# Two decoder layers on one core: gate and up of every feed-forward group token-major, the activations turned in squares of 32 and sent round by DRAM

## The chip, the cores and the metric

The kernel runs as one program on one core of a Trainium2 chip. Its time is the device time of one execution in microseconds (us); a comparison uses the median of several executions. A profile is one further execution, recorded by the hardware profiler; its span is the stretch from the first to the last recorded work.

## The reference

Two layers of a decoder trunk on 256 tokens of width 1024, all in fp32. Each layer has two feed-forward blocks (FFN), so the kernel runs four of them, and the change lies in these:

```python
D_MODEL, SEQ, DEPTH, D_FF = 1024, 256, 2, 2816

def swiglu(x, w_gu, w_down):
    gate, up = jnp.split(x @ w_gu, 2, axis=-1)      # (256, 2816) each
    return (jax.nn.silu(gate) * up) @ w_down        # (256, 1024)

def hybrid_layer(...):
    h = layer_norm(ALPHA * x + 0.5 * swiglu(x, ffn1_w_gu, ffn1_w_down), ...)
    # token mixers on h @ w_in: gated DeltaNet, sliding-window attention, memory cross-attention
    ...
    h = layer_norm(ALPHA * h + merged @ w_out, ...)
    return layer_norm(ALPHA * h + 0.5 * swiglu(h, ffn2_w_gu, ffn2_w_down), ...)
```

## The kernel before

**Precision.** Every large product is made of three float32r products. An operand x is split into hi (a cast, on ScalarE, `split` L116) and lo = x - hi (a subtraction, on VectorE, L117); the product is hi*hi + hi*lo + lo*hi (`mm3`).

**The weight stream.** All weights lie in one DRAM array `wst` in the order of use. `unit` takes the next 128 x 1024 piece (512 KB): a DMA on SP's queue into one of 3 `raw` buffers, then the split into one of 5 pairs `whi`, `wlo`. The buffers set how far the stream runs ahead: a new DMA starts when VectorE has done with a `raw` buffer, a new cast when TensorE has done with a `whi` buffer.

**PSUM.** The pool `acc` has four banks of 128 x 512, used in turn.

**An FFN.** The 2816 gate and 2816 up columns go in 22 tiles of 128, or 11 groups of 256 (group i holds tiles 2i and 2i + 1). Group 0 is made ahead of the rest, by `both` (first FFN) or `first` (the other three), token-major: for each block tb of 128 tokens one bank holds 256 gate and 256 up columns, the activations hT are the stationary operand and 512 weight columns move. `first_out` then applies silu, multiplies, turns the 128 x 256 result by two TensorE transposes and splits it into the tile `u0`. Tiles 2 to 21 go through `shares`, feature-major: 128 weight columns are stationary and the activations move. hT holds hi and lo side by side (128 x 512), so `whi` times both is one matmul of 512 columns, and `wlo` times hi is one of 256. For every k of 8 and for gate and up that makes 2 matmuls of 512 and 2 of 256. Two copies and two additions join the halves of the banks (L183, L184), then come silu (L372), the product (L374) and the split into `u`. The result is feature-major, as the down projection wants its stationary operand, and nothing leaves the core for it. The down projection (`projA`) reads 22 units and accumulates into all four `acc` banks and one more.

**Order.** A scheduler of the recording layer orders each engine's instructions by priorities; the loads on SP's queue keep program order. An engine executes its instructions in the order recorded, so an instruction that waits holds back all that stand behind it on that engine. GpSimd (POOL) is idle in the FFN but for eight DMAs of the memory rows (`mdr`, L431 and L435). In the token mixers it issues the DMAs `dr<-t` and `w<-dr`, which send a tile round by DRAM.

Of the kernel before, what the change touches and what calls it, by code (L numbers as in the profile page):

```python
# [38 lines left out]
def tile_trunk(ctx, tc, x, xT, mem, wst, lnp, memln, cvw, rows, cst, out):  # L39
    nc = tc.nc  # L40
# [5 lines left out]
    p2 = ctx.enter_context(tc.tile_pool(name="p2", bufs=2))  # L46
# [4 lines left out]
    pd = ctx.enter_context(tc.tile_pool(name="pd", bufs=2, space=bass.MemoryType.DRAM))  # L51
    uid = [0]

    def nm(s):
        uid[0] += 1
        return f"{s}_{uid[0]}"

    def T(pool, shape, tag, dt=F32, bufs=None):
        kw = {} if bufs is None else {"bufs": bufs}
        return pool.tile(shape, dt, tag=tag, name=nm(tag), **kw)  # L60

    def acc():
        return T(psA, [P, 512], "acc")
# [4 lines left out]
    def sm():  # L68
        return T(psS, [P, 512], "sm")
# [6 lines left out]
    ident = cs[:, C_ID:C_ID + P]  # L76
# [22 lines left out]
    def unit(w=U, dst=None, cuts=1, behind=None):  # L99
        ahead = tc.high_priority(offset=AHEAD) if pos[0] >= 8 * P * U else nullcontext()  # L100
        raw = T(praw, [P, U], "raw")
        src = wst[pos[0]:pos[0] + P * w].rearrange("(p w) -> p w", p=P)
        pos[0] += P * w
        (ph, th), (pl, tl) = dst or ((phi, "whi"), (plo, "wlo"))
        with ahead:
            hi = T(ph, [P, U], th, F32R)
            lo = T(pl, [P, U], tl, F32R)
            for i in range(cuts):
                c = slice(i * w // cuts, (i + 1) * w // cuts)
                nc.sync.dma_start(raw[:, c], src[:, c])  # L110
                with tc.issue_after(behind) if behind else nullcontext():
                    split(hi[:, c], lo[:, c], raw[:, c])
        return hi, lo

    def split(hi, lo, src):
        nc.scalar.copy(hi, src)  # L116
        return nc.vector.tensor_tensor(lo, src, hi.bitcast(F32), op=ALU.subtract).ins  # L117
# [3 lines left out]
    def pe(ins):  # L121

        return tc.keep_in_program_order(ins) if pinned[0] else ins

    def matmul(*a, **k):
        return pe(nc.tensor.matmul(*a, **k))  # L126
# [4 lines left out]
    def mm3(o, l, r, first, last, skip=False):  # L131
        (lh, ll), (rh, rl) = l, r
        matmul(o, lh, rh, start=first, stop=False, skip_group_check=skip)
        matmul(o, lh, rl, start=False, stop=False, skip_group_check=skip)
        matmul(o, ll, rh, start=False, stop=last, skip_group_check=skip)
# [28 lines left out]
            yield  # L164
        return banks

    def shares(hT, behind=None):


        banks = [acc() for _ in range(2)]  # L170
        for uu in range(2):
            hi, lo = unit(behind=behind)
            for kk in range(4):
                k = uu * 4 + kk
                cs_ = [slice((kk * 2 + t) * P, (kk * 2 + t + 1) * P) for t in range(2)]

                for t in range(2):
                    matmul(banks[t], hi[:, cs_[t]], hT[2][:, k], start=k == 0, stop=False, skip_group_check=True)
                for t in range(2):
                    matmul(banks[t][:, 0:S], lo[:, cs_[t]], hT[0][:, k, :], start=False, stop=k == KD - 1, skip_group_check=True)  # L180
        y = T(p2, [P, 2, S], "t2", bufs=4)
        for t in range(2):
            nc.scalar.copy(y[:, t], banks[t][:, S:])  # L183
            nc.vector.tensor_tensor(y[:, t], y[:, t], banks[t][:, 0:S], op=ALU.add)  # L184
        return y

    def halves(xt, use):

        for i in range(2):
            (b,) = yield from projB_parts(xt, 2, 4)  # L190
            use(i, b)
# [42 lines left out]
    def full_rows():  # L234

        a, b, c, d = (acc() for _ in range(4))
        return [[a, b], [c, d[:, 0:S], at()[:, 0:S]]]
# [8 lines left out]
    def new_hT():  # L246

        t = T(pu, [P, KD, 2, S], "hT", F32R)
        return t[:, :, 0, :], t[:, :, 1, :], t
# [64 lines left out]
    class Ffn:  # L314
# [27 lines left out]
        def both(self, hT):  # L342
            self.bank = {tb: acc() for tb in range(2)}
            for k in range(KD):
                hi, lo = self.units[k // 2]
                c = slice((k % 2) * 512, (k % 2) * 512 + 512)
                for tb in range(2):
                    ts = slice(tb * P, (tb + 1) * P)
                    mm3(self.bank[tb], (hT[0][:, k, ts], hT[1][:, k, ts]), (hi[:, c], lo[:, c]), k == 0, k == KD - 1)
            for tb in range(2):  # L350
                self.first_out(tb)

        def first_out(self, tb):
            ps = self.bank[tb]
            hf = self.glu(ps[:, 0:S], ps[:, S:2 * S])
            pt = sm()
            for j in range(2):
                nc.tensor.transpose(pt[:, j * P:(j + 1) * P], hf[:, j * P:(j + 1) * P], ident)
            ts = slice(tb * P, (tb + 1) * P)
            split(self.h(0)[:, 0, :, ts], self.h(0)[:, 1, :, ts], pt[:, 0:S].rearrange("p (j t) -> p j t", j=2))  # L360

        def glu(self, g, u):
            sg = T(p2, [P, S], "t2", bufs=4)
            nc.scalar.activation(sg, g, AF.Silu)
            hf = T(p2, [P, S], "t2", bufs=4)
            nc.vector.tensor_tensor(hf, sg, u, op=ALU.mult)
            return hf

        def rest(self, hT, tail, dsts, post, mid={}, behind=None):
            for f in range(2, NFT):  # L370
                y = shares(hT, behind if f == 2 else None)
                nc.scalar.activation(y[:, 0], y[:, 0], AF.Silu)  # L372
                hf = y[:, 1]
                nc.vector.tensor_tensor(hf, y[:, 0], hf, op=ALU.mult)  # L374
                t = self.h(f // 2)
                split(t[:, 0, f % 2, :], t[:, 1, f % 2, :], hf)
                if f in mid:
                    mid[f]()
            outs = full_rows()
            projA((lambda k: self.hu[k // 2][:, 0, k % 2, :], lambda k: self.hu[k // 2][:, 1, k % 2, :]), D, 1, NFT, outs, tail, dsts, after=post)  # L380

# [32 lines left out]
    def begin(nxt, hT):  # L414
        nxt.first(hT, 0)
        nxt.first(hT, 1)
        nxt.first_out(0)
        nxt.first_out(1)


    mdr = T(pd, [4, P, 1024], "mdr", bufs=1)
# [569 lines left out]
    hT = new_hT()  # L991
# [20 lines left out]
    for l in range(NL):  # L1012
        mT = []
        mid = memory_T(mT, l)
# [16 lines left out]
        if not last:  # L1031
            f1, hT = Ffn(), post.hT
# [4 lines left out]
def _kcols(w, kpu):  # L1037

    k = w.shape[0] // P
    return np.ascontiguousarray(w.reshape(k // kpu, kpu, P, w.shape[1]).transpose(0, 2, 1, 3)).ravel()  # L1040


def _stream(i):
    parts = []
    for l in range(NL):
        def ffn(gu, dn):
            parts.append(_kcols(np.concatenate([gu[:, 0:S], gu[:, FF:FF + S]], 1), 2))
            g = gu.reshape(KD // 4, 4, P, 2, NFT, P)
            parts.append(np.ascontiguousarray(g[:, :, :, :, 2:].transpose(4, 0, 2, 1, 3, 5)).ravel())
            parts.append(_kcols(dn, 1))  # L1050
        ffn(i["ffn1_w_gu"][l], i["ffn1_w_down"][l])
        mk = i["w_mem_kv"][l]
        parts.append(_kcols(mk[:, :512], 2))
        parts.append(_kcols(mk[:, 512:], 2))
        w = i["w_in"][l]
        parts.append(_kcols(np.concatenate([w[:, 1536:2056], w[:, 2696:2824]], 1), 1))
        for s in (512, 0, 1024, 2824):
            parts.extend(_kcols(w[:, c:c + 256], 4) for c in (s, s + 256))
        parts.append(_kcols(w[:, 2568:2696], 8))
        sq = w[:, 2056:2568].reshape(D, 2, 4, 64).transpose(0, 2, 1, 3).reshape(D, 512)  # L1060
        parts.extend(_kcols(sq[:, s:s + 256], 4) for s in (0, 256))
        wb = i["w_branch"][l]
# [57 lines left out]
```

## Time and profile before

| | us |
|---|---|
| median of 3 runs (1297.15 to 1299.23) | 1298.52 |
| the profiled execution | 1298.02 |
| its span | 1296.2 |
| what lies around the span | 1.8 |
| TensorE busy in it | 1277.9 |
| VectorE, ScalarE, GpSimd busy | 888.4, 708.5, 77.2 |

A timeline row gives start, duration, engine, source line, operation, output<-inputs (moving operand ahead of the stationary one for a matmul), the shape and how many instructions were merged. A matmul's duration includes its way through the array and overlaps the next one; what a matmul costs is the distance from start to start. In a row of instruction groups the two numbers behind the first bar are the busy time in us and the mean of one in ns; behind the second stands the idle time ahead of them, with what ended it.

### The profile page before, as it was taken

The page shows a single profiled execution, that of the slowest core. Times are in us where ns is not written, and L with a number is a line of the kernel's source. Part 1 is how long each engine was busy: PE and PEld are TensorE (multiplying, and loading weights), DVE is VectorE, ACT ScalarE, POOL GpSimd, SP SyncE. Part 2 cuts the span into 40 slices and gives each one's busy share as a digit, 9 for nine tenths or more (in the row PEclk, how much of TensorE's full clock was granted, in tenths as well). Part 3 has the DMA queues.
Part 4 walks back from the last instruction along what each step waited for, and adds up shares of the span by engine and source line. Part 5 has one row for each costly group of instructions (what it writes and reads, how often), then busy time and mean ns, then how long its engine had stood idle before and what let it go on. Part 6 is the DMA issues. An engine that isn't in the chain of part 4 may idle for free.

```text
span 1296.2 us, 20444 instructions
## 1 busy us (share of the span) xinstructions
PE 1277.9 (99%) x7832; PEld 1116.2 (86%) x7832; DVE 888.4 (69%) x1430; ACT 708.5 (55%) x1177; POOL 77.2 (6%) x135
## 2 busy tenths in 40 slices
PE   8999999999999999999999999999999999999997
PEld 6888889999878888888888888899988788888886
DVE  6787556796647777665677674759867388777645
ACT  6656444666674546554455654456656654565541
POOL 0000000102311000000000000000033100000000
PEclk9999999999999999999999999999999999999999
DMA  7867564654533636555665555556453256455553
GB/s 266 276 210 244 193 229 128 220 174 135 161 131 130 228 129 211 191 185 192 228 222 200 188 186 192 199 175 201 163 165 131 98 182 224 149 194 194 189 189 111
DMA packets 68577, 240.25 MB, mean 185 GB/s; under 512 B 8160, under 2 KB 9312, under 8 KB 68480
## 3 DMA queue, kind: packets, MB, share of 16 engines
q1 hardware_dynamic: 66176, 232.53, 53.1%
q0 software_dynamic: 2304, 6.43, 1.8%
q8 instruction: 61, 1.00, 0.3%
q14 instruction: 36, 0.29, 0.1%
HBM read 235.64 MB, written 3.28 MB: 184 GB/s over the span
## 4 chain that ended last, share of the span: by engine, by line
PE 89%; DVE 4%; DMA 4%; ACT 2%; issue 1%; SPq 0%; DVEq 0%; ACTq 0%
PE acc L126 78%; PE at L126 4%; DMA raw<-in_wst_dram 3%; PE sm L126 3%; PE sm L129 1%; ACT whi L116 1%; DVE wlo L117 1%; PE acc L340 1%; PE acc L337 1%; DMA pp<-in_mem_dram 1%; PE acc L338 1%; PE at L129 1%; DVE bnst L282 0%; DVE u L117 0%; DVE h L301 0%
## 5 line engine op out<-in xcount | busy, mean ns | idle before, releaser
L117 DVE TENSOR_TENSOR wlo<-raw,whi 128x1024 fp32r<-128x1024 f32 (+2 forms) x403 | 487.4, 1214 | 308.7 <-ACT whi L116 307.2
L116 ACT CAST whi<-raw 128x1024 fp32r<-128x1024 f32 (+2 forms) x403 | 414.4, 1033 | 366.7 <-DMA raw<-in_wst_dram 99.0
L126 PE MATMUL acc<-hT,whi 128*128 128x512 f32 (+1 forms) x1952 | 524.9, 357 | 0.0
L126 PEld LDWEIGHTS acc<-hT,wlo 128*128 128x128 f32 x1616 | 304.6, 189 | 56.0
L126 PE MATMUL acc<-hT,wlo 128*128 128x256 f32 x1616 | 347.6, 279 | 0.0
L126 PEld LDWEIGHTS acc<-hT,whi 128*128 128x128 f32 x1952 | 299.8, 190 | 0.2
L126 PE MATMUL acc<-whi,u 128*128 128x512 f32 (+1 forms) x800 | 246.7, 373 | 0.0
L126 PEld LDWEIGHTS acc<-whi,u 128*128 128x128 f32 x800 | 150.1, 188 | 27.7 <-DVE t L184 1.2
L126 PE MATMUL acc<-whi,hT 128*128 128x512 f32 (+1 forms) x544 | 168.4, 380 | 5.6 <-ACT whi L116 5.6
L126 PE MATMUL acc<-wlo,u 128*128 128x512 f32 (+1 forms) x400 | 148.4, 371 | 0.0
L126 PEld LDWEIGHTS acc<-whi,hT 128*128 128x128 f32 x544 | 100.6, 189 | 23.7 <-ACT whi L116 5.6
L126 PE MATMUL acc<-wlo,hT 128*128 128x512 f32 (+1 forms) x272 | 101.9, 375 | 0.0
L126 PEld LDWEIGHTS acc<-wlo,u 128*128 128x128 f32 x400 | 75.5, 189 | 12.2
L372 ACT ACTIVATE t<-t 128x256 f32<-128x256 f32 x80 | 33.4, 417 | 60.4 <-DVE t L184 59.9
L184 DVE TENSOR_TENSOR t<-t,acc 128x256 f32<-128x256 f32 x160 | 59.9, 415 | 0.0
L126 PEld LDWEIGHTS acc<-wlo,hT 128*128 128x128 f32 x272 | 51.5, 190 | 8.2 <-DVE wlo L117 0.9
L183 ACT COPY t<-acc 128x256 f32<-128x256 f32 x160 | 51.5, 369 | 0.1
L116 ACT CAST u<-t 128x256 fp32r<-128x256 f32 x80 | 32.1, 401 | 20.4 <-DVE t L374 20.4
L374 DVE TENSOR_TENSOR t<-t 128x256 f32<-128x256 f32 x80 | 33.9, 424 | 9.2 <-ACT t L372 7.7
L126 PE MATMUL at<-whi,u 128*128 128x256 f32 x152 | 39.0, 283 | 0.0
L117 DVE TENSOR_TENSOR u<-t,u 128x256 fp32r<-128x256 f32 x80 | 33.6, 420 | 7.1 <-ACT u L116 7.1
L489 DVE SCALAR_TENSOR_TENSOR t<-acc,cw,t 128x255 f32<-128x255 f32 (+2 forms) x72 | 34.5, 479 | 0.9
(248 smaller groups left out, 1250.4 us busy)
## 6 DMA issues: line engine op xcount, KB each, us to landing
raw<-in_wst_dram SPq DMA_DIRECT2D x409, 512.0 KB, 3.6
raw<-in_wst_dram SPq DMA_DIRECT2D x16, 324.0 KB, 3.0
gB<-in_lnp_dram SPq DMA_DIRECT2D x6, 512.0 KB, 6.4
bB<-in_lnp_dram SPq DMA_DIRECT2D x6, 512.0 KB, 5.9
mdr<-w POOLq DMA_DIRECT2D x4, 512.0 KB, 6.8
w<-dr POOLq DMA_DIRECT2D x4, 512.0 KB, 8.8
w<-mdr POOLq DMA_DIRECT2D x4, 512.0 KB, 5.2
t<-in_xT_dram SPq DMA_DIRECT2D x4, 256.0 KB, 5.3
```

The costliest lines, as they stand in the source:

```text
L116: nc.scalar.copy(hi, src)
L117: return nc.vector.tensor_tensor(lo, src, hi.bitcast(F32), op=ALU.subtract).ins
L126: return pe(nc.tensor.matmul(*a, **k))
L129: return pe(nc.tensor.transpose(*a))
L183: nc.scalar.copy(y[:, t], banks[t][:, S:])
L184: nc.vector.tensor_tensor(y[:, t], y[:, t], banks[t][:, 0:S], op=ALU.add)
L337: nc.tensor.matmul(ps, hT[0][:, k, ts], hi[:, c], start=k == 0, stop=False)
L338: nc.tensor.matmul(ps, hT[0][:, k, ts], lo[:, c], start=False, stop=False)
L340: nc.tensor.matmul(ps, hT[1][:, k, ts], hi[:, c], start=False, stop=k == KD - 1)
L372: nc.scalar.activation(y[:, 0], y[:, 0], AF.Silu)
L374: nc.vector.tensor_tensor(hf, y[:, 0], hf, op=ALU.mult)
L489: nc.vector.scalar_tensor_tensor(yc[:, j, d:], b[:, j, :S - d], w[:, t:t + 1], yc[:, j, d:], op0=ALU.mult, op1=ALU.add)
```

## The change

All groups are now made as group 0 was, token-major, with 512 weight columns moving: per k and token block the three matmuls of `mm3`. `shares` is gone. For each group the new `out` makes silu and product of both token blocks into one tile t, which holds 32 columns of block 0 beside the same 32 columns of block 1, and so on. VectorE then transposes every 32 x 32 square of t in place of TensorE (L341). That leaves the four bands of 32 partitions each with the wrong quarter of the tokens; four DMAs of GpSimd's queue write the bands to a DRAM tile `tr`, 64 KB each in pieces of 512 bytes (L345), and a fifth, which waits for the four, reads it back with 2 KB to a partition (L346). The result y is split into `u`. The rows of the down weights are reordered on the host to fit, and so is the stream; the number and size of the stream's units are the same, and SP's queue stands in the same order.

```diff
-    def shares(hT, behind=None):
-        banks = [acc() for _ in range(2)]
-        for uu in range(2):
-            hi, lo = unit(behind=behind)
-            for kk in range(4):
...
-                for t in range(2):
-                    matmul(banks[t], hi[:, cs_[t]], hT[2][:, k], start=k == 0, stop=False, skip_group_check=True)
-                for t in range(2):
-                    matmul(banks[t][:, 0:S], lo[:, cs_[t]], hT[0][:, k, :], start=False, stop=k == KD - 1, skip_group_check=True)
...
+            self.out(0, self.bank)
+
+        def out(self, i, banks):
+            t = T(p2, [P, 8, 2, 32], "t2", bufs=4)
             for tb in range(2):
-                self.first_out(tb)
...
+                g, u = (banks[tb][:, c:c + S].rearrange("p (j x) -> p j x", j=8) for c in (0, S))
+                nc.scalar.activation(t[:, :, tb, :], g, AF.Silu)
+                nc.vector.tensor_tensor(t[:, :, tb, :], t[:, :, tb, :], u, op=ALU.mult)
+            z = T(p2, [P, 512], "t2", bufs=4)
+            nc.vector.transpose(z, t.rearrange("p j t x -> p (j t x)"))
+            y = T(p2, [P, 512], "t2", bufs=4)
+            d = T(pd, [4, 32, 4, P], "tr")
+            for q in range(4):
+                nc.gpsimd.dma_start(d[:, :, q].rearrange("b c x -> c b x"), z[32 * q:32 * q + 32].rearrange("c (b x) -> c b x", b=4))
+            nc.gpsimd.dma_start(y, d.rearrange("b c q x -> (b c) (q x)"))
+            hi, lo = (self.h(i)[:, n].rearrange("p a (t q s) -> p (a t) q s", t=2, q=4) for n in range(2))
+            split(hi, lo, y.rearrange("p (q n s) -> p n q s", q=4, n=4))

         def rest(self, hT, tail, dsts, post, mid={}, behind=None):
-            for f in range(2, NFT):
-                y = shares(hT, behind if f == 2 else None)
-                nc.scalar.activation(y[:, 0], y[:, 0], AF.Silu)
...
+            for i in range(1, NFT // 2):
+                banks = [acc() for _ in range(2)]
+                for uu in range(KD // 2):
+                    hi, lo = unit(behind=behind if i == 1 and uu < 2 else None)
+                    for kk in range(2):
+                        k, c = 2 * uu + kk, slice(kk * 512, kk * 512 + 512)
+                        for tb in range(2):
+                            ts = slice(tb * P, (tb + 1) * P)
+                            mm3(banks[tb], (hT[0][:, k, ts], hT[1][:, k, ts]), (hi[:, c], lo[:, c]), k == 0, k == KD - 1)
+                self.out(i, banks)
```

In the orders below a number behind a name is the buffer; rows are of the second FFN (end of layer 0). ScalarE before, tiles 12 and 13: the copies, the silu and the cast of one tile, then the next.

```order
L183 COPY t_929_5491<-acc_5445 128x256
L183 COPY t_929_5491<-acc_5446 128x256
L372 ACTIVATE t_929_5491<-t_929_5491 128x256
L116 CAST whi_5637<-raw_5636 128x1024
L116 CAST u_930_5498<-t_929_5491 128x256
L116 CAST whi_5670<-raw_5669 128x1024
L183 COPY t_939_5547<-acc_5501 128x256
```

Each cast into `u` reads what the same engine and VectorE have just made. ScalarE now, group 9 and the start of group 10 (t_971 is the y of group 8, t_988 the t of group 9):

```order
L338 ACTIVATE t_988_5488<-acc_5414 128x8x32
L116 CAST whi_5602<-raw_5601 128x1024
L116 CAST u_973_5411<-t_971_5404 128x512
L338 ACTIVATE t_988_5488<-acc_5415 128x8x32
L116 CAST whi_5623<-raw_5622 128x1024
L116 CAST whi_5644<-raw_5643 128x1024
L116 CAST whi_5665<-raw_5664 128x1024
L338 ACTIVATE t_1007_5579<-acc_5505 128x8x32
```

The cast of group 8's y, which waits for a DMA, now stands between the two silus of group 9. VectorE before, tile 14 of that FFN:

```order
L184 TENSOR_TENSOR t_948_5602<-t_948_5602,acc_5556 128x256
L184 TENSOR_TENSOR t_948_5602<-t_948_5602,acc_5557 128x256
L374 TENSOR_TENSOR t_948_5602<-t_948_5602 128x256
L117 TENSOR_TENSOR wlo_5749<-raw_5747,whi_5748 128x1024
L117 TENSOR_TENSOR u_949_5609<-t_948_5602,u_949_5609 128x256
L117 TENSOR_TENSOR wlo_5782<-raw_5780,whi_5781 128x1024
```

The residual into `u` belongs to the tile just made. VectorE now, groups 9 and 8:

```order
L339 TENSOR_TENSOR t_988_5488<-t_988_5488,acc_5414 128x8x32
L117 TENSOR_TENSOR wlo_5603<-raw_5601,whi_5602 128x1024
L117 TENSOR_TENSOR u_973_5411<-t_971_5404,u_973_5411 128x512
L339 TENSOR_TENSOR t_988_5488<-t_988_5488,acc_5415 128x8x32
L341 STREAM_TRANSPOSE t_989_5493<-t_988_5488 128x512
L117 TENSOR_TENSOR wlo_5624<-raw_5622,whi_5623 128x1024
```

The residual of group 8 stands ahead of group 9's second product and of its transpose. GpSimd now, groups 8, 9 and 10 (nothing stood here before):

```order
L345 DMA tr_5405<-t_970_5402 32x4x128 x4
L346 DMA t_971_5404<-tr_5405 128x512
L345 DMA tr_5496<-t_989_5493 32x4x128 x4
L346 DMA t_990_5495<-tr_5496 128x512
L345 DMA tr_5587<-t_1008_5584 32x4x128 x4
L346 DMA t_1009_5586<-tr_5587 128x512
```

t_971 and t_990 are the y of groups 8 and 9, which ScalarE casts; each read stands behind its four writes, and the next group's writes behind it. TensorE now, just behind the second FFN's group 10: the start of its down projection, from the seventh matmul on (six into `acc_5596` and `acc_5597` stand ahead):

```order
L126 MATMUL acc_5598<-whi_5602,u_821_4683 128x512
L126 MATMUL acc_5598<-wlo_5603,u_821_4683 128x512
L126 MATMUL acc_5598<-whi_5602,u_821_4683 128x512
L126 MATMUL at_5600<-whi_5602,u_821_4683 128x256
L126 MATMUL at_5600<-wlo_5603,u_821_4683 128x256
L126 MATMUL at_5600<-whi_5602,u_821_4683 128x256
L126 MATMUL acc_5596<-whi_5623,u_821_4683 128x512
L126 MATMUL acc_5596<-wlo_5624,u_821_4683 128x512
L126 MATMUL acc_5596<-whi_5623,u_821_4683 128x512
L126 MATMUL acc_5597<-whi_5623,u_821_4683 128x512
L126 MATMUL acc_5597<-wlo_5624,u_821_4683 128x512
L126 MATMUL acc_5599<-whi_5602,u_821_4683 128x256
```

`acc_5598` and `acc_5599` take the two banks of group 10. So 17 matmuls, 14 of 512 columns and 3 of 256, stand between the end of group 10 and the first into `acc_5599`, which can start only when VectorE has read group 10's second bank for its second product.

More of the change, by code (lines that the diff above doesn't have):

```diff
@@ L165, in projB_parts @@
         return banks
-    def shares(hT, behind=None):
-        banks = [acc() for _ in range(2)]
-        for uu in range(2):
-            hi, lo = unit(behind=behind)
-            for kk in range(4):
-                k = uu * 4 + kk
-                cs_ = [slice((kk * 2 + t) * P, (kk * 2 + t + 1) * P) for t in range(2)]
-                for t in range(2):
-                    matmul(banks[t], hi[:, cs_[t]], hT[2][:, k], start=k == 0, stop=False, skip_group_check=True)
-                for t in range(2):
-                    matmul(banks[t][:, 0:S], lo[:, cs_[t]], hT[0][:, k, :], start=False, stop=k == KD - 1, skip_group_check=True)
[L181 to L185, printed above, removed]
     def halves(xt, use):
@@ L349, in both @@
                     mm3(self.bank[tb], (hT[0][:, k, ts], hT[1][:, k, ts]), (hi[:, c], lo[:, c]), k == 0, k == KD - 1)
+            self.out(0, self.bank)
+        def out(self, i, banks):
+            t = T(p2, [P, 8, 2, 32], "t2", bufs=4)
             for tb in range(2):
-                self.first_out(tb)
[L353 to L367, printed above, removed]
-        def rest(self, hT, tail, dsts, post, mid={}, behind=None):
-            for f in range(2, NFT):
-                y = shares(hT, behind if f == 2 else None)
[L372 to L378, printed above, removed]
+                g, u = (banks[tb][:, c:c + S].rearrange("p (j x) -> p j x", j=8) for c in (0, S))
@@ new lines, in out @@
+            nc.gpsimd.dma_start(y, d.rearrange("b c q x -> (b c) (q x)"))
+            hi, lo = (self.h(i)[:, n].rearrange("p a (t q s) -> p (a t) q s", t=2, q=4) for n in range(2))
+            split(hi, lo, y.rearrange("p (q n s) -> p n q s", q=4, n=4))
+        def rest(self, hT, tail, dsts, post, mid={}, behind=None):
+            for i in range(1, NFT // 2):
[8 more added lines that the diff above has]
+                self.out(i, banks)
+                for f in (2 * i, 2 * i + 1):
+                    if f in mid:
+                        mid[f]()
@@ L416, in begin @@
         nxt.first(hT, 1)
-        nxt.first_out(0)
-        nxt.first_out(1)
+        nxt.out(0, nxt.bank)
     mdr = T(pd, [4, P, 1024], "mdr", bufs=1)
@@ L1046, in ffn @@
         def ffn(gu, dn):
[L1047 to L1050, printed above, removed]
+            for c in range(0, FF, S):
+                parts.append(_kcols(np.concatenate([gu[:, c:c + S], gu[:, FF + c:FF + c + S]], 1), 2))
+            parts.append(_kcols(dn.reshape(FF // S, 4, 2, 32, D).transpose(0, 2, 1, 3, 4).reshape(FF, D), 1))
         ffn(i["ffn1_w_gu"][l], i["ffn1_w_down"][l])
```

## Prediction

> **What bounds the kernel now.** I read the page's head, the granted clock, the chain and then TensorE's waits.
>
> ```profile
> span 1296.2 us, 20444 instructions
> PE 1277.9 (99%) x7832; PEld 1116.2 (86%) x7832; DVE 888.4 (69%) x1430; ACT 708.5 (55%) x1177; POOL 77.2 (6%) x135
> PEclk9999999999999999999999999999999999999999
> PE 89%; DVE 4%; DMA 4%; ACT 2%; issue 1%; SPq 0%; DVEq 0%; ACTq 0%
> PE acc L126 <- ACT whi L116: 5.6, 1, 5.6
> PE sm L129 <- DVE h L301: 1.9, 4, 1.0
> ```
>
> TensorE is busy 99% of the span at full clock, and 89% of the chain is its own. The last two rows are the longest of its waits: the first is the start of the kernel, and nothing behind it adds up to more than a few us. So two things count: how long TensorE's own instructions take, and whether the change makes it wait. The work taken from ScalarE and VectorE (copies, additions) is worth nothing by itself, since TensorE hides it already.
>
> **TensorE's stream.** A timeline of TensorE gives each form's price from start to start. The first two rows are the first and last whole k of the second FFN's `shares` behind its transposes, 153 k apart; the next two are the form that the change uses everywhere (hT stationary, weights moving, in the order of `both`), 27 matmuls apart.
>
> ```profile
> 480.65 0.63 PE L126 MATMUL acc<-hT,whi 128*128 128x512 f32 x2
> 587.24 0.63 PE L126 MATMUL acc<-hT,whi 128*128 128x512 f32 x2
> 11.60 0.63 PE L126 MATMUL acc<-whi,hT 128*128 128x512 f32 x2
> 17.73 0.62 PE L126 MATMUL acc<-whi,hT 128*128 128x512 f32 x2
> 475.90 0.38 PE L358 MATMUL sm<-cs,t 128*128 128x128 f32 x2
> 476.03 0.71 PE L126 MATMUL acc<-hT,whi 128*128 128x512 f32 x2
> ```
>
> A k of one tile costs 106.59/153 = 0.697 us (2 matmuls of 512 columns and 2 of 256), so a group, two tiles of 8 k, costs 11.15 us. A matmul of the new form costs 6.13/27 = 0.227 us, so a group of 8 k x 2 blocks x 3 costs 10.90 us. The columns are equal (24576); what falls is the number of matmuls, 64 to 48. That is 0.25 us for each of 40 groups: 10.0 us. `first_out`'s transposes go too: 0.13 us from 475.90 to 476.03, and from there to 480.65 pass 4.62 us for 6 k, which would take 4.18. That is 0.57 us an FFN, 2.3 in four. TensorE's own gain: 12.3 us.
>
> **What the path by DRAM costs.** Call R the time from the end of VectorE's transpose to the landing of y. No row shows such a trip; its parts have rows. The first six are from timelines of ScalarE, GpSimd and VectorE, the next four from the table of issues and from single lines, the last from stretches of 0.5 us (its last column is GB/s), while only `w<-mdr` ran.
>
> ```profile
> 107.88 0.59 ACT L116 CAST w<-sm 128x512 fp32r<-128x512 f32 x1 [0.16 <-PE sm L129]
> 107.75 0.76 POOL L435 DMA_DIRECT2D mdr<-w  x1 [106.91 <-ACT t L183]
> 108.77 1.60 POOL L435 DMA_DIRECT2D mdr<-w  x3 [0.26 <-ACT w L116]
> 107.02 1.22 DVE L117 TENSOR_TENSOR wlo<-raw,whi 128x1024 fp32r<-128x1024 f32 x1
> 315.94 0.60 POOL L726 DMA_DIRECT2D dr<-t  x1
> 319.55 1.22 POOL L730 DMA_DIRECT2D w<-dr  x2 [3.00 <-DMA dr<-t]
> dr<-t POOLq DMA_DIRECT2D x2, 64.0 KB, 3.0
> w<-mdr POOLq DMA_DIRECT2D x4, 512.0 KB, 5.2
> DMA to landing us min/median/max: 3.7/5.2/6.8
> w<-dr POOLq DMA_DIRECT2D x4, 512.0 KB, 8.8
> 650.50:651.00 0.50, 0.50 (x4) 0.39 (x3) 0.50 (x2) 0.50 (x2) 0.00 (x0) 1.00 1.14 410
> ```
>
> An engine's result releases a DMA of GpSimd 0.30 us later (108.47 to 108.77). An issue takes 0.53 to 0.76 us; at 0.60 the fourth starts 1.8 us after the first. A 64 KB write followed by a DMA that waits for it takes 3.61 us from issue to issue (315.94 to 319.55). The read of 256 KB: the quickest read by DRAM of 512 KB landed 3.7 us after its issue; half of it is 0.65 us less at 410 GB/s, so 3.05. Sum 8.76, and I add 0.25 for the weight stream beside it: R = 9.0. The ends: 0.30 + 1.60 + 3.55 + 2.95 = 8.4 with nothing in the way; 0.30 + 2.3 + 3.6 + 4.55 = 10.75 with issues of 0.76 and the read at its median. The row of 8.8 us, a read that repeats its source, I leave as an outer bound.
>
> **The loop that this closes.** The orders show what stands behind y. VectorE makes the residual of group i-1 ahead of the second product and the transpose of group i, and ScalarE has the cast ahead of the second silu. So y of group i cannot set out before y of group i-1 has landed:
>
> ```profile
> L116 ACT CAST u<-acc 128x512 fp32r<-128x512 f32 x12 | 6.9, 577 | 0.0
> L117 DVE TENSOR_TENSOR hT<-sm,hT 128x512 fp32r<-128x512 f32 x20 | 12.9, 676 | 0.0
> L372 ACT ACTIVATE t<-t 128x256 f32<-128x256 f32 x80 | 33.4, 417 | 60.4 <-DVE t L184 59.9
> L374 DVE TENSOR_TENSOR t<-t 128x256 f32<-128x256 f32 x80 | 33.9, 424 | 9.2 <-ACT t L372 7.7
> L788 DVE STREAM_TRANSPOSE w<-w x4: 297/306/312, 364.6 to 1005.1; 128x128 f32<-128x128 f32 x4
> L837 DVE STREAM_TRANSPOSE w<-w x2: 445/446/446, 343.1 to 983.1; 128x256 f32<-128x256 f32 x2
> L117 DVE TENSOR_TENSOR wlo<-raw,whi 128x1024 fp32r<-128x1024 f32 x385 | 472.8, 1233 | 289.9 <-ACT whi L116 288.3 <-PE acc L126 0.5
> L116 ACT CAST whi<-raw 128x1024 fp32r<-128x1024 f32 x385 | 401.4, 1048 | 348.4 <-DMA raw<-in_wst_dram 96.9 <-PE at L126 81.8 <-PE acc L126 80.5
> ```
>
> Cast 0.58, residual 0.68, product 0.42, transpose of 512 columns 0.73 (0.31 for 128, 0.14 for each 128 more), 0.1 for the first release: 2.5 us. The loop is R + 2.5 = 11.5 us, against TensorE's 10.9 a group: each group comes out 0.6 us later.
>
> Start with the FFNs 2 to 4, whose orders are alike. From the end of group 1 pass its silu (0.42 us), a weight cast (1.05), the `wlo` behind it (1.23), group 0's residual (0.68) and the transpose (0.73): 4.1 us. So y of group 1 lands 13.1 us after, 2.2 us after the end of group 2. Eight loops bring y of group 9 to 94.2 us after the end of group 2; group 10 ends 8 x 10.9 = 87.2 us after it, so y is 7.0 us late. Cast, residual and product (1.7) free group 10's second bank at 8.7. TensorE wants it 14 x 0.227 + 3 x 0.12 = 3.55 us after that end (a matmul of 256 columns is half of 0.697 - 2 x 0.227). It waits 5.15 us at the start of each of three down projections: 15.4 us. Until then nothing stops: group i+2 needs the banks of group i only one group later, and the weight casts behind the wait have a group's lead in the five buffers. R goes nine times into that wait (once, and eight loops), so 0.1 us more or less is worth 2.7 us of the kernel.
>
> In FFN 1 the orders break the loop twice (transposes 3 and 8 stand ahead of the residuals 2 and 7), but the `mdr` DMAs stand between group 7's writes and its read. Between nothing and the others' 5 us I take 2.
>
> A wait of 5 us may cool TensorE. The one idle stretch of that length is the start:
>
> ```profile
> 5.62 0.80 PE L126 MATMUL acc<-whi,hT 128*128 128x512 f32 x1 [5.62 <-ACT whi L116]
> 8.97 0.40 PE L126 MATMUL acc<-wlo,hT 128*128 128x512 f32 x1
> ```
>
> Seven matmuls took 3.35 us instead of 1.6: 1.75 lost. Between none and 1.75 for each of three waits I take the upper value, as 5.15 us is nearest to that row's 5.6: 5.
>
> Two things cost nothing. The trips add 23 MB (44 x 512 KB) of traffic to 240 MB that keep the DMA engines busy for 55% of the span:
>
> ```profile
> DMA packets 68577, 240.25 MB, mean 185 GB/s; under 512 B 8160, under 2 KB 9312, under 8 KB 68480
> q1 hardware_dynamic: 66176, 232.53, 53.1%
> q0 software_dynamic: 2304, 6.43, 1.8%
> ```
>
> And silu, product, transpose and split are fewer instructions than the copies, additions and splits that they replace, on engines that TensorE hides; if that cover goes, it is by the loop above.
>
> **Sum.** Profiled execution 1298.0 - 12.3 + 15.4 + 2 + 5 = 1308 us. That execution lies 0.5 us below the median shown, which is nothing here. A change under 0.2% (2.6 us) cannot be told from none.
>
> **The rivals.**
>
> *The trip is hidden; faster.* At R = 8.4 the loop is 10.9 us, TensorE's own pace, and the wait is gone: 1298.0 - 12.3 = 1286 us. It decides where the three waits fall below 12.3 - 2 us, 3.4 each, without cooling: R below 8.8. For it: my uncrowded sum is 8.76, and writes and reads may meet an idle stream, since the stalled VectorE frees no `raw` buffer. Against it: every surcharge goes the other way. [...]
>
> *GpSimd is held up by VectorE; slower still.* The `mdr` issue that ran under a `wlo` (107.02 to 108.24) took 0.76 us, the three behind it 0.53 each. All four writes follow a transpose, behind which three `wlo` stand on VectorE. With 0.76 for each issue R grows by 0.6, the three waits by 16 us: 1324 us. One row is little evidence. [...]
>
> *Small pieces are slow; much slower.* The writes go in pieces of 512 bytes to scattered places; `dr<-t` wrote a solid block. At R = 10.75 the loop is 13.25 us and the waits are 21 us in each of three FFNs and 5 in the first: 1298 - 12.3 + 62 + 5 + 5 = 1358 us.
>
> **Chances.** Forecast (1301 to 1320) 0.40; GpSimd held up, up to 1335: 0.10; beyond that 0.10; within 0.2% of before 0.09; faster, 1286 to 1295: 0.31. Hence faster 0.31, same 0.09, slower 0.60. The range 1286 to 1335 leaves out the one in ten above. The forecast's own range is 1301 to 1320.
>
> **What would show it.** Right: in the profile after, TensorE's matmuls into `acc` stand 0.227 us apart, L358 and L184 are gone, ScalarE waits for a DMA ahead of each `u` cast, and TensorE waits at the start of the down projections for VectorE's L339, some 5 us in three of four. Writes issue 0.6 us apart and the y lands about 3 us behind its issue. Wrong: no such wait on TensorE (the trip is shorter), a wait inside the groups (it is far longer), or a start-to-start other than 0.227.

## The result, and the profile after

The changed kernel takes 1370.62 us (median of 4 runs, 1368.23 to 1371.55) against 1297.97 us before: a ratio of 1.0556, 95% interval 1.0538 to 1.0574. It is 72.6 us slower; 1308 was forecast, with 1301 to 1320 as the forecast's own range. The head of the page after, and then the two largest entries of TensorE's waits (total us, times, longest):

```profile
span 1368.8 us, 19252 instructions
PE 1290.0 (94%) x7176; PEld 1099.4 (80%) x7176; DVE 850.7 (62%) x1270; ACT 652.6 (48%) x973; POOL 197.1 (14%) x355
PEclk9999999999999999998999998999999999999899
```

```profile
PE acc L126 <- DVE t L339: 51.1, 24, 6.2
PE sm L129 <- DVE pp L281: 7.9, 1, 7.9
```

TensorE idles 78.8 us of the span instead of 18.3. The wait is for VectorE's product (L339), which frees a bank, as forecast, but it comes 24 times, within the groups too and not at the down projections alone. The second row was not forecast: the transposes of the normed memory rows in the first FFN. The loss lies in the FFNs. Measured at the last matmul into `at` of each down projection, the four stretches that end there grew by 17.2, 18.6, 17.1 and 19.7 us; of that the token mixers between them make under 1 us each.

One group of the second FFN, from timelines of VectorE, GpSimd and ScalarE, shows the loop:

```profile
561.29 0.71 DVE L341 STREAM_TRANSPOSE t<-t 128x512 f32<-128x512 f32 x1
562.30 2.17 POOL L345 DMA_DIRECT2D tr<-t  x4 [5.18 <-DVE t L341]
568.78 0.57 POOL L346 DMA_DIRECT2D t<-tr  x1 [4.31 <-ACT whi L116]
571.83 0.62 ACT L116 CAST u<-t 128x512 fp32r<-128x512 f32 x1 [3.42 <-DMA t<-tr]
572.48 0.69 DVE L117 TENSOR_TENSOR u<-t,u 128x512 fp32r<-128x512 f32 x1 [2.81 <-ACT u L116]
573.54 0.71 DVE L341 STREAM_TRANSPOSE t<-t 128x512 f32<-128x512 f32 x1
```

From transpose to transpose pass 12.25 us: 9.83 from the end of the first to the cast (R), and 2.42 for cast, residual, product and transpose. The cast starts when y has landed and everything behind it runs without a gap, so one trip sets out only when the one before is done. (The read's row names a `whi` cast that ended 0.37 us before it. But in 39 of the 44 trips the read starts 0.5 to 0.7 us behind the landing of the last write, so it waits for the writes.) TensorE's matmuls of a group take 10.88 us, so each group comes 1.37 us later than TensorE could take it.

R was forecast at 9.0. Its median over the groups 2 to 8 of FFNs 2 to 4 is 9.74: 0.30 for the release as forecast, 6.48 from the first write's issue to the read's issue (forecast 1.8 + 3.61 = 5.41), 3.03 from there to the cast (forecast 3.05 + 0.25). The last trip of the first FFN, which set out right behind a wait of TensorE's while hardly any weight was moving (66 to 131 GB/s from 154 to 157 us, the writes included), took 4.25 us for the same step. Two rows of GpSimd's timeline, and two of the table of issues (median us to landing in the last column):

```profile
153.51 2.18 POOL L345 DMA_DIRECT2D tr<-t  x4 [5.14 <-DVE t L341]
157.76 0.57 POOL L346 DMA_DIRECT2D t<-tr  x1 [2.08 <-ACT whi L116]
```

```profile
tr<-t POOLq DMA_DIRECT2D x176, 64.0 KB, 3.7
t<-tr POOLq DMA_DIRECT2D x44, 256.0 KB, 3.2
```

So the writes look slow beside the weight stream only. And the loop brings the stream upon them itself. Three `wlo` stand behind the transpose on VectorE, and each frees a `raw` buffer as it ends; so weight loads set out at 563.14, 564.27 and 565.41 us, 0.84, 1.97 and 3.11 us behind the first write. Here are SP's row, which merges these loads and a later one, and three stretches (length, GpSimd's busy time with its instructions, granted clock, DMA share, GB/s):

```profile
563.14 6.89 SPq L110 DMA_DIRECT2D raw<-in_wst_dram  x4
560.30:562.30 2.00, 0.00 (x1) 1.00 0.07 27
562.30:564.30 2.00, 2.00 (x4) 1.00 0.36 68
564.30:566.30 2.00, 0.17 (x1) 1.00 0.94 256
```

The first write went out with no load under way and landed after 2.0 us; the fourth took 4.2 us. In the median of the groups above the four took 2.0, 3.3, 4.2 and 4.2 us.

At the start of the second FFN's down projection TensorE waits three times. These are its timeline and stretches of 2 us (stretch, length, TensorE's busy time with its instructions, granted clock, DMA share, GB/s):

```profile
610.67 0.50 PE L126 MATMUL acc<-whi,u 128*128 128x512 f32 x1 [1.16 <-DVE t L339]
615.12 0.80 PE L126 MATMUL acc<-whi,u 128*128 128x512 f32 x1 [3.48 <-DVE t L339]
625.61 0.58 PE L126 MATMUL acc<-whi,u 128*128 128x256 f32 x1 [6.17 <-DVE t L339]
```

```profile
616.00:618.00 2.00, 2.00 (x7) 0.50 0.99 334
626.00:628.00 2.00, 2.00 (x7) 0.50 0.16 33
```

Behind the two longer waits TensorE works at half clock for some 4 us (615.1 to 619.2 and 625.6 to 629.4). Summed over stretches of 0.5 us, the busy time times what the clock lacked is 20.8 us in the whole kernel, in ten places, 1.6 to 3.0 us each.

### The profile page after: what moved, and what is told of

Same layout as the page of the kernel before. It is cut to its first block, busy times and chain, and to the rows that moved or that the text cites. A ratio compares the mean times of both kernels' runs of the same rounds, so it can differ in the third digit from the quotient of the medians.

```text
span 1368.8 us, 19252 instructions
## 1 busy us (share of the span) xinstructions
PE 1290.0 (94%) x7176; PEld 1099.4 (80%) x7176; DVE 850.7 (62%) x1270; ACT 652.6 (48%) x973; POOL 197.1 (14%) x355
## 5 line engine op out<-in xcount | busy, mean ns | idle before, releaser
L126 PE MATMUL acc<-whi,hT 128*128 128x512 f32 (+1 forms) x1824 | 571.2, 389 | 25.1 <-DVE t L339 20.3
L126 PEld LDWEIGHTS acc<-whi,hT 128*128 128x128 f32 x1824 | 342.9, 189 | 99.9 <-DVE t L339 26.6
L126 PE MATMUL acc<-wlo,hT 128*128 128x512 f32 (+1 forms) x912 | 352.5, 387 | 0.3 <-DVE wlo L117 0.3
L126 PEld LDWEIGHTS acc<-wlo,hT 128*128 128x128 f32 x912 | 172.8, 189 | 33.2 <-DVE wlo L117 1.2
L345 POOL DMA_DIRECT2D tr<-t x176 | 96.1, 553 | 414.6 <-DVE t L341 407.7
L126 PE MATMUL acc<-hT,whi 128*128 128x256 f32 x672 | 122.3, 284 | 0.0
L126 PEld LDWEIGHTS acc<-hT,whi 128*128 128x128 f32 x672 | 104.7, 192 | 0.0
L126 PE MATMUL acc<-hT,wlo 128*128 128x256 f32 x336 | 95.0, 283 | 0.0
L126 PEld LDWEIGHTS acc<-wlo,u 128*128 128x128 f32 x400 | 78.8, 197 | 13.0
L126 PEld LDWEIGHTS acc<-hT,wlo 128*128 128x128 f32 x336 | 64.4, 192 | 0.0
L346 POOL DMA_DIRECT2D t<-tr x44 | 25.0, 568 | 184.9 <-DMA tr<-t 139.6
L339 DVE TENSOR_TENSOR t<-t,acc 128x256 f32<-128x256 f32 x88 | 35.9, 414 | 3.5 <-ACT t L338 3.3
L338 ACT ACTIVATE t<-acc 128x256 f32<-128x256 f32 x88 | 32.6, 378 | 3.0 <-PE acc L126 3.0
## 6 DMA issues: line engine op xcount, KB each, us to landing
w<-dr POOLq DMA_DIRECT2D x4, 512.0 KB, 10.4
```

What stands on the lines that cost most here:

```text
L338: nc.scalar.activation(t[:, :, tb, :], g, AF.Silu)
L339: nc.vector.tensor_tensor(t[:, :, tb, :], t[:, :, tb, :], u, op=ALU.mult)
L345: nc.gpsimd.dma_start(d[:, :, q].rearrange("b c x -> c b x"), z[32 * q:32 * q + 32].rearrange("c (b x) -> c b x", b=4))
L346: nc.gpsimd.dma_start(y, d.rearrange("b c q x -> (b c) (q x)"))
```

## The experiments

The theory: the loop, one trip for each group that waits for the one before, costs the time, and the trip is longer than forecast because the weight stream runs beside it. The rivals: the trips' traffic itself slows the weight stream; the trip is long whatever runs beside it; its small pieces make it long.

### The same DMAs without the loop

```diff
+            if self.fin:
+                with tc.issue_after(si), tc.issue_after(tr):   # second silu, transpose
+                    self.fin()                                 # split of group i - 1
+            def fin():
                 hi, lo = (self.h(i)[:, n].rearrange(...) for n in range(2))
                 split(hi, lo, y.rearrange("p (q n s) -> p n q s", q=4, n=4))
+            self.fin = fin
```

> The changed kernel with the same DMAs, but the cast and residual that turn y of group i-1 into u are queued behind the second silu and the transpose of group i, so that no trip waits for the one before. Theory A (the loop: each trip sets out only after the one before has landed; 12.25 us a group in the profile of the changed kernel against 10.9 us of TensorE's work): the loop is gone, the trip of 9.8 us fits into a group, all waits of TensorE for banks (51 us) and the half clock behind them (some 20 us) go, and what is left is TensorE's own gain: 1298 - 12.3 = 1286 us, 1284 to 1290. Rival B (the trips' 23 MB and their DMAs slow the weight stream, ScalarE's waits for raw having risen from 99 to 220 us): traffic is unchanged, the time stays near 1370 us, above 1340.

Measured: 1302.45 us (1298.24 to 1305.06, 10 runs), 1.0032 of before (1.0018 to 1.0046). TensorE's waits in its profile, and one group of the second FFN:

```profile
PE sm L129 <- DVE pp L281: 4.7, 1, 4.7
PE acc L126 <- DVE t L339: 3.5, 3, 1.9
```

```profile
564.03 0.71 DVE L341 STREAM_TRANSPOSE t<-t 128x512 f32<-128x512 f32 x1
565.03 2.17 POOL L345 DMA_DIRECT2D tr<-t  x4 [3.90 <-DVE t L341]
565.76 0.62 ACT L116 CAST u<-t 128x512 fp32r<-128x512 f32 x1 [3.08 <-DMA t<-tr]
574.99 0.71 DVE L341 STREAM_TRANSPOSE t<-t 128x512 f32<-128x512 f32 x1
```

The transposes now stand 10.96 us apart, and the cast comes behind the next transpose. The order alone gave back 68 us, with every byte still sent: the loop is shown, and traffic is not the bulk. But 1286 was missed by 16 us. In the profiled execution, one of the longer ones (1305.06 us), the second and third stretch are 2.3 and 2.1 us shorter than before; the first is 8.5 us longer, the last 3.0. In the first FFN ScalarE still waited 8.1 us for y between 10 and 90 us, and the memory rows, whose loads stand in SP's queue behind the weights, were late (the first was issued at 72.76 us, against 66.80 before): TensorE waited 4.7 and then 2.7 us ahead of their transposes, and worked at half clock behind each (from 90 to at least 95 us, and from 109.3 to 112.8).

### No trip at all

```diff
-            y = T(p2, [P, 512], "t2", bufs=4)
-            d = T(pd, [4, 32, 4, P], "tr")
...
-            nc.gpsimd.dma_start(y, d.rearrange("b c q x -> (b c) (q x)"))
+            y = z
```

> The changed kernel without the path by DRAM: u is made straight from VectorE's transpose z, so the output is not the reference's; the five DMAs of each group are left out, everything else stays. It shows what the new matmul form is worth by itself. Both theories: no waits for banks, 1298 - 12.3 = 1286 us. If TensorE's gain was mis-sized it shows here: 10 us less than 1286 or more than it would say so. The distance to the kernel with the deferred splits is what the hidden trips still cost: theory A 0 to 3 us, rival B some 60 us.

Measured: 1288.58 us (1287.16 to 1289.33), 0.9930 of before (0.9913 to 0.9946); the profiled span is 10.8 us shorter than before, and no wait of TensorE for L339 is left. So the matmul form is worth about what was forecast (12.3 us) or slightly less, and the trips cost 82 us in the changed kernel and 14 us with the splits deferred by one group, where 0 to 3 were expected.

### A thin weight stream, the order as it was

```diff
+            if thin:                                   # groups 1 to 10
+                nc.sync.dma_start(raw[:, 0:S], src[:, 0:S])
+                ... split(h4, l4, raw[:, 0:S].unsqueeze(1).to_broadcast([P, 4, S]))
```

> The changed kernel with its order as it is, but of each 512 KB weight unit of groups 1 to 10 only the first 128 KB is loaded, and the splits read these four times over (so the output is not the reference's). Theory A with the trip lengthened by the weight stream (first write to read issue 6.4 us with the stream beside it, 4.2 us for the last trip of an FFN, when the stream stood still): the trip shrinks to 0.3 + 4.2 + 2.9 = 7.4 us, the loop to 9.9 us, below TensorE's 10.9, and the time comes to 1286 to 1295 us. Rival C (the trip is long by itself, through four queued issues and its small pieces, whatever runs beside it): the trip stays near 9.8 us, the loop at 12.2 and the time above 1350 us.

Measured: 1312.32 us (one run). One group of the second FFN, the writes in the table of issues, and TensorE's longest wait (lines were added ahead, so that the product is L345 here):

```profile
535.09 0.71 DVE L347 STREAM_TRANSPOSE t<-t 128x512 f32<-128x512 f32 x1
536.10 2.17 POOL L351 DMA_DIRECT2D tr<-t  x4 [6.12 <-DVE t L347]
543.65 0.61 ACT L122 CAST u<-t 128x512 fp32r<-128x512 f32 x1
545.97 0.71 DVE L347 STREAM_TRANSPOSE t<-t 128x512 f32<-128x512 f32 x1
```

```profile
tr<-t POOLq DMA_DIRECT2D x176, 64.0 KB, 2.2
```

```profile
PE acc L132 <- DVE t L345: 17.1, 4, 6.4
```

R is 7.85 us at most: the cast's row shows no wait, and y had landed some 0.2 us before it. The writes land in 2.2 us instead of 3.7, and the groups stand 10.88 us apart, TensorE's own pace: the stream beside the writes was the mis-sized cost. The time did not reach 1295. The units of the down projection were left whole and are loaded during the last groups; there R grew to 10.4 and 13.1 us, and the four waits in the last row stand at the start of the four down projections. With 7.6 us at half clock they make 24.7 us, about the 23.7 between this kernel and the one without a trip.

### The small pieces on the other side

```diff
+            d = T(pd, [4, 32, 512], "tr")
+            nc.gpsimd.dma_start(d.rearrange("q c w -> (q c) w"), z)
+            for b in range(4):
+                nc.gpsimd.dma_start(y[32 * b:32 * b + 32]..., d[:, :, P * b:P * b + P].rearrange("q c x -> c q x"))
```

> The changed kernel with the small pieces moved from the writes to the reads: one write of 256 KB in rows of 2 KB, then four reads of 64 KB in pieces of 512 bytes; the order of the other engines stays. Theory A says that the time follows the trip, by 4 FFNs x 10 groups = some 40 us for each us of trip beyond the 8.4 us at which the loop equals TensorE's 10.9. If the four issues ahead of the wait are the cost, the write phase falls by 1.6 us and the read phase grows by 1.6, R stays near 9.8 us and the time near 1370. If pieces of 512 bytes are slow in writes alone, R falls by 1 us or more, to 8.8 us or less, and the time to 1330 us or less; if reads in such pieces are slower than writes, R grows and the time lies above 1390 us.

Measured: 1394.18 us (one run). Its table of issues, and one group:

```profile
tr<-t POOLq DMA_DIRECT2D x44, 256.0 KB, 2.4
t<-tr POOLq DMA_DIRECT2D x176, 64.0 KB, 5.8
```

```profile
577.98 0.71 DVE L341 STREAM_TRANSPOSE t<-t 128x512 f32<-128x512 f32 x1
581.94 2.17 POOL L346 DMA_DIRECT2D t<-tr  x4 [2.39 <-issue]
588.77 0.62 ACT L116 CAST u<-t 128x512 fp32r<-128x512 f32 x1 [3.40 <-DMA t<-tr]
590.48 0.71 DVE L341 STREAM_TRANSPOSE t<-t 128x512 f32<-128x512 f32 x1
```

One write of 256 KB landed sooner than four of 64 KB, and the four reads took longer than the one. The write is issued at 578.99 us and has landed by 581.4; the first load that a `wlo` sets off is issued at 579.83, so the write is nearly done when the stream comes, like the first of the four. The median R is 10.82 and the period 13.24 us, again R + 2.42. The time grew by 23.6 us for 1.08 us of R, 22 us for each (27 in the forecast, 40 in the expectation). This is the expectation's third case.

### Four writes in long rows: the order moved by itself

```diff
             for q in range(4):
-                nc.gpsimd.dma_start(d[:, :, q].rearrange("b c x -> c b x"), z[32 * q:32 * q + 32]...)
-            nc.gpsimd.dma_start(y, d.rearrange("b c q x -> (b c) (q x)"))
+                nc.gpsimd.dma_start(d[q], z[32 * q:32 * q + 32])
+            for b in range(4):
+                nc.gpsimd.dma_start(y[32 * b:32 * b + 32]..., d[:, :, P * b:P * b + P].rearrange("q c x -> c q x"))
```

> The changed kernel with four writes of 64 KB in rows of 2 KB and four reads of 64 KB in pieces of 512 bytes; between this and the kernel with one write only the number of writes differs. If the length of a piece decides how long a DMA takes beside the weight stream, the writes land 2 to 2.5 us after their issue (3.7 in pieces of 512 bytes), the read phase is that of the kernel with one write (7.5 us from the first read's issue to the cast), R grows from 10.8 to 12 us, the loop to 14.4 us, and the time by some 25 us for each us of R, to 1425 us. If four DMAs are slow as such, the writes keep their 3.7 us and the time lies above 1440 us.

Measured: 1333.15 us (one run), far below either number, with the longest trip of all, 13.3 us in the median. The reason stands in VectorE's order. With eight DMAs on a trip the scheduler of the recording layer placed the residual of group i-1 behind the transpose of group i, throughout FFNs 2 to 4, as the first experiment does by hand:

```
L341 STREAM_TRANSPOSE t_875_4989<-t_874_4984 128x512
L117 TENSOR_TENSOR u_859_4907<-t_857_4897,u_859_4907 128x512
```

The timeline shows it (the cast of the trip before comes 3 us behind a transpose, and the next transpose does not wait for it), and the table of issues shows the writes:

```profile
515.13 0.71 DVE L341 STREAM_TRANSPOSE t<-t 128x512 f32<-128x512 f32 x1
518.84 0.62 ACT L116 CAST u<-t 128x512 fp32r<-128x512 f32 x1 [3.25 <-DMA t<-tr]
524.94 0.71 DVE L341 STREAM_TRANSPOSE t<-t 128x512 f32<-128x512 f32 x1
```

```profile
tr<-t POOLq DMA_DIRECT2D x176, 64.0 KB, 3.5
t<-tr POOLq DMA_DIRECT2D x176, 64.0 KB, 4.6
```

A trip of 13.3 us in this order costs 37 us less than one of 9.7 us in the other: the order decides, not the length. The writes landed in 3.5 us though their rows are 2 KB long. In the first experiment, which has the residual in the same place, pieces of 512 bytes took 3.1 us:

```profile
tr<-t POOLq DMA_DIRECT2D x176, 64.0 KB, 3.1
```

So the length of a piece is not what makes the four writes slow. What the number of DMAs costs by itself is not separated here: with another order other loads run beside them.

### The turn by TensorE

```diff
+                hf = T(p2, [P, S], "t2", bufs=4)
...
+                for j in range(2):
+                    nc.tensor.transpose(pt[:, j * P:(j + 1) * P], hf[:, j * P:(j + 1) * P], ident)
+                split(self.h(i)[:, 0, :, ts], self.h(i)[:, 1, :, ts], pt[:, 0:S]...)
```

> The other half of the change alone: all groups token-major with 512 weight columns, but each turned by TensorE as the kernel before turns group 0 (two transposes of 128 x 128 for each token block, then the split), with nothing sent to DRAM; the down weights keep their old order. TensorE gains 10.0 us by the matmuls and pays four transposes of 0.13 us for each of 40 groups, 0.52 x 40 = 20.8 us: 1309 us, if the transposes find their operands ready. If they stall TensorE's queue (a silu, a product and a split lie between), 1315 us or more.

Measured: 1317.24 us (1315.77 to 1322.83), 1.0167 of before (1.0139 to 1.0195). The first transposes of two neighbouring groups in TensorE's timeline, and its waits for them:

```profile
562.03 0.40 PE L342 MATMUL sm<-cs,t 128*128 128x128 f32 x2
573.54 0.39 PE L342 MATMUL sm<-cs,t 128*128 128x128 f32 x2
```

```profile
PE sm L342 <- DVE t L339: 3.0, 4, 1.4
```

A group takes 11.51 us, 0.63 more than its matmuls alone (0.52 expected), and TensorE waited 3.0 us for a product, so transposes cost more than the matmul form gains. The time is that of the expectation's second case (1315 or more): 0.63 us for each of 40 groups, less the 10 us gained, and the waits make 18 of the 20 us.

### Splits deferred by two groups

```diff
+            if len(self.fins) == 2:
+                with tc.issue_after(si), tc.issue_after(pr):   # second silu, second product
+                    self.fins.pop(0)()                         # split of group i - 2
```

> As the kernel with deferred splits, but the split of group i-2 stands behind the second product of group i and ahead of its transpose, with five t2 buffers in place of four: a trip has two groups, some 20 us, instead of one. With a deferral of one group three FFNs already ran at TensorE's pace, but the trips of 12 to 15 us in the first FFN, and two of 14 us at the end of the last one, were longer than a group; in the first FFN the memory rows were loaded 7.9 us later than in the kernel without a trip (72.8 against 64.9 us), TensorE waited 7.4 us for their layer norm and ran at half clock behind each wait. Theory A: with 20 us for a trip these go too, and the time comes to that of the kernel without a trip, 1288.6 us, at most 1292. Rival (the trips' traffic delays the first FFN's loads whatever waits for them): FFN 1 stays as with one group, 1298 to 1303 us.

Measured: 1294.08 us (1290.67 to 1294.76), 0.9970 of before (0.9958 to 0.9982). The time lies between the two cases (at most 1292, or 1298 and more). The stretches 2 to 4 are 3.3, 3.2 and 3.3 us shorter than before, at least as much as without a trip (3.2, 3.2 and 0.9); the first is 3.4 us longer, where it is 3.6 us shorter without a trip. (The next expectation has 6.3 us for this difference of 6.9, and 20 for the start of the stretch below.) Here are ScalarE's waits between 10 and 90 us, of the kernel without a trip and of this one, and TensorE's wait:

```profile
ACT whi L116 <- DMA raw<-in_wst_dram: 11.8, 12, 1.7
```

```profile
ACT whi L116 <- DMA raw<-in_wst_dram: 31.8, 23, 3.0
```

```profile
PE sm L129 <- DVE pp L281: 4.0, 1, 4.0
```

ScalarE no longer waits for y there, only for weights. So in the first FFN the rival is right as far as these rows go: SP's queue also carries `x`, the memory rows and their gains there, and with the trips' traffic the loads come later.

### The memory rows' norm one group later

```diff
-        return {13: again} if l else {11: vecs, 13: lambda: rows_(0), 15: lambda: rows_(1), 16: keep}
+        return {13: again} if l else {11: vecs, 13: lambda: fetch(0), 15: lambda: (fetch(1), rows_(0)), 17: lambda: rows_(1), 18: keep}
```

> The kernel with splits deferred by two groups, and in the first FFN the layer norms of the memory rows and the transposes behind them stand one group later; their loads stay where they were in SP's order. In the kernel with two groups, FFN 1 was the only stage behind the kernel without a trip (6.3 us): its loads ran late (ScalarE waited 31.8 us for raw between 20 and 90 us, against 11.8 without a trip, and not at all for y), TensorE waited 4.0 us for the normed memory rows and lost 3.0 us at half clock behind that. If that wait is all that the traffic costs, it goes: 1294.1 - 7 = 1287 us. If the weights themselves come too late in FFN 1, TensorE waits for whi instead, and the time stays at 1291 to 1295 us.

Measured: 1292.48 us (1290.05 to 1292.9), 0.9956 of before (0.9942 to 0.9970), the fastest with all of the work in it; its interval and that of the version with two groups overlap. TensorE's longest wait for a bank, at its place:

```profile
136.24 0.79 PE L126 MATMUL acc<-whi,u 128*128 128x512 f32 x1 [4.72 <-DVE t L339]
```

The wait for the memory rows is gone and one of the same size stands at the start of the first down projection, with 3.1 us at half clock behind it; a silu stood behind a weight cast that waited 0.95 us for `raw`. The first stretch ends at 199.36 us, against 199.27 before this edit and 192.35 without a trip. The wait moved: some 7 us in the first FFN stay while the trips run, and 1287 was wrong. The time is that of the second case, though TensorE waited for a bank and not for `whi`.

## Why the prediction was wrong, point by point

**TensorE's own gain, 12.3 us: right.** Without a trip TensorE's busy time falls by 12.8 us (1277.9 to 1265.1), and a group takes 10.88 us (10.90 forecast). The kernel is 9.5 us faster by the medians (7.0 to 11.3) and 10.8 by the profiles, since idle time rises by 2.0.

**The loop: right, and its formula R + 2.5 too.** Three kernels in the same order give a period of 10.88 (R at most 7.85, a loop below TensorE's pace), 12.16 (9.74) and 13.24 us (10.82).

**R = 9.0: the term that was mis-sized, at the writes.** The surcharge of 0.25 us for "the weight stream beside it" was set by eye, between ends whose lower one had "nothing in the way". The writes took 6.48 us from the first issue to the read's with the stream and 4.40 with a quarter of it. The prediction allowed that they might meet an idle stream, since the stalled VectorE frees no `raw` buffer. That held for the first write alone; VectorE's three `wlo` behind the transpose then set off the loads that the other three met. Issues were 0.54 us each, and the read was priced right. The missing 0.74 us are worth 20 us by the forecast's own slope.

**"Until then nothing stops": wrong.** A wait of 5.15 us at the start of each of three down projections was forecast. At 1.3 us a group the lead of the banks was used up in mid-FFN, and TensorE waited some 1 us in each group behind; at the start of the second and third FFN's down projections it waited for three banks in turn. Some trips beside the loads of the down weights were longer (the one that begins at 610.65 us took 12.52 us to its cast). The booked waits of FFNs 2 to 4 are 45 us, where 15.4 were forecast and 35 follow from R = 9.74. Each short wait also cost about 0.3 us beyond the time booked (12.25 us from transpose to transpose, less 10.88 and a wait of 1.06).

**"Cooling", 5 us: the price was near, the count was not.** A stretch at half clock cost 1.6 to 3.0 us, against 1.75 taken from the kernel's start; there were ten, not three. In the ten places TensorE worked 3.2 to 6.0 us at half clock. How long a wait must be to bring that on is not shown: the last section has a wait of 3.24 us without it and one of 1.79 us with it.

**FFN 1, 2 us: wrong.** The order broke the loop three times there (the residuals of groups 0, 2 and 7 stand behind the next transpose), and still it lost as much as the others. Its trips were the longest in the median (11.5 us, against 9.7 to 9.9 in the others), where more than weights is loaded, and through VectorE's late residuals and `raw` the memory rows came late: TensorE's 7.9 and 1.8 us in front of L129, and behind both half clock (1.8 and 1.7 us lost).

**"The traffic costs nothing": right in three FFNs, wrong in the first,** where about 7 us remain with every wait for y gone.

**The rivals.** GpSimd was not held up: its four issues took 2.17 us in the loop above, with `wlo` on VectorE beside them, and over the whole trace an issue took 0.55 us in the median with a `wlo` running and without one. The rival of small pieces came nearest to the time (1358) by a cause that the runs speak against. The hidden trip needed R below 8.8. The runs show at most 7.85 with a thin stream beside the trip and 9.74 with the real one.

Together, as estimates from these rows: 20 us by R, 10 by the waits that R does not explain, 18 in the first FFN, 9 by half clock in the others, and 7 for restarts. They come to 64 us, near the 62.6 between 1308 and 1370.6. Why the booked waits exceed what the median R gives is explained only in part, by the longer trips beside the down weights.

## What to carry to other kernels

When a result is sent on a long trip, look at what stands in front of the next departure on the engines that start it: a wait for the last arrival there turns a latency into a rate (here R + 2.42 us a group). Queue what waits for the arrival behind the next departure, and the trip may take a whole group longer at a small part of the cost (here the order alone gave back 68 of 82 us). Price a DMA beside the stream that will run beside it, not from a quiet place (here the writes took 6.48 us with the stream and 4.40 with a quarter of it). Ask, too, what stands behind the departure and what it sets off: here it was the very loads that the trip then met. And price the traffic separately in the stage whose loads are densest (here some 7 us stayed in the first FFN).

## What the runs showed of the hardware

- Writes of 64 KB, four in a row on GpSimd's queue, landed 3.7 us after their issue in the changed kernel and 2.2 us beside a quarter of the weight stream. The first of the four, issued with no load under way, took 2.0 us in the median, the last two 4.2 us. One write of 256 KB, issued 0.84 us ahead of the loads, took 2.4 us. Long rows did not help (3.5 us, against 3.1 in pieces of 512 bytes, the residual in the same place).
- The length of a wait alone does not tell whether the clock falls. In the changed kernel a wait of 3.24 us left it whole, and one of 1.79 us was followed by 3.4 us at half clock, from 110.6 to 114.0 us (the two waits, then stretches of 2 us):

```profile
791.32 0.50 PE L126 MATMUL acc<-whi,hT 128*128 128x512 f32 x1 [3.24 <-DVE t L339]
109.47 0.63 PE L129 MATMUL sm<-cs,pp 128*128 128x128 f32 x4 [1.79 <-issue]
```

```profile
792.00:794.00 2.00, 2.00 (x11) 1.00 0.16 33
112.00:114.00 2.00, 2.00 (x6) 0.50 0.75 193
```
